# Expert layer on one core: the second expert matrix loaded by whole rows, its products regrouped, one output bank for each expert

## The chip, the cores and the metric

The kernel runs on one core of one Trainium2 chip. The metric is the device time of one execution in microseconds (us); lower is better. A program on one core has one TensorE, one VectorE (DVE), one ScalarE (ACT), one GpSimd (POOL), one SyncE (SP, which here issues most DMAs) and 16 DMA engines.

## The reference

The whole program is two transformer blocks on 256 tokens of 1024 features, float32. The change touches only its last part, the mixture of experts of the second block. There are 16 experts; each picks its 32 best tokens.

```python
def expert_choice_moe(h, p):
    cap = EC_CAPACITY * T // N_EXPERTS
    affinity = jax.nn.softmax((h @ p['router_w']).astype(jnp.float32), axis=-1)
    gates, idx = lax.top_k(jnp.swapaxes(affinity, 1, 2), cap)
    xe = jax.vmap(lambda hb, ib: hb[ib])(h, idx)
    hid = jax.nn.silu(jnp.einsum('becd,edf->becf', xe, p['exp_w1'])) * jnp.einsum('becd,edf->becf', xe, p['exp_w3'])
    ye = jnp.einsum('becf,efd->becd', hid, p['exp_w2']) * gates[..., None].astype(h.dtype)
    return jax.vmap(lambda ib, yb: jnp.zeros((T, D), yb.dtype).at[ib.reshape(-1)].add(yb.reshape(-1, D)))(idx, ye)
```

Here `exp_w1` and `exp_w3` are [1024, 2048] for each expert and `exp_w2` is [2048, 1024]. Each of the three is 8 MB, so the 16 experts read 384 MB. After the sum comes a norm of the rows, a gain, and the addition to the block's input.

## The kernel before, in words

The part in question is the function `moe` (lines 1589 to 1838). It runs after the attention block, two dense feed-forward blocks and the second mixer. Weights stay in HBM until they are used; each load of them is one DMA of 1 MB, issued by SP in `wload` (L1764), into a slot of 8 KB on each of the 128 partitions. There are 19 slots, used in turn (`RINGS`, `RING_ORDER`, `slot`), and a slot is loaded again once TensorE has used what it held. The loads of one expert are eight of `exp_w1`, eight of `exp_w3` and eight of `exp_w2`, in that order, expert after expert: 384 in all. They all go through SP's one queue in the order of the program.

For one expert, in the order of the work:

- L1779: products with `exp_w1`, then with `exp_w3`. A load holds 128 rows of 2048 numbers, one whole row of 8 KB on each partition. Four matmuls use it, one for each group g of 512 hidden columns; the stationary operand is the expert's 32 gathered tokens (`xeT`), so each matmul takes 32 columns of TensorE's array, and the four stand side by side and fill the 128 partitions of a PSUM bank: partition 32 g + token, column = hidden column inside the group.
- L1790 to L1792: silu and the gating product, on ACT and DVE, into `th` (the trace calls it mth) of 128 x 512.
- L1795 and L1797: four transposes on TensorE bring the hidden columns onto partitions (`hid`); block q takes the 128 columns q * 128 to q * 128 + 127 of every group.
- L1802 and L1804: the matrix that puts the 32 results back to their tokens with their gates, repeated four times over the 128 partitions (`pgT`).
- L1812: products with `exp_w2`, first for output columns 0 to 511, then for 512 to 1023 (`nh`). A load for half `nh` and block q takes, on each partition, four pieces of 512 numbers (2 KB): the half row of hidden column q * 128 + p of each of the four groups. Four matmuls use it, one for each group, into four groups of 32 partitions of one PSUM bank.
- L1815 and L1817: when a half is done, ACT copies the bank to SBUF (`ye`), and two matmuls, one for each half of the tokens, add it to the output sums in PSUM (`acc[t][nh]`). Their contraction over 128 partitions also adds the four groups.

```python
wv = A["exp_w2_2"][e].rearrange("(g q p) n -> q p g n", g=4, q=4)      # before
for nh in range(2):
    ns = slice(nh * 512, nh * 512 + 512)
    pe2 = psT.tile([128, 512], F32, name="tr")
    for q in range(4):
        w2t = wload(wv[q, :, :, ns], 512)
```

After the last expert come the squares of the four sums on ACT and their product with the gain on DVE (in the loop over nh, then t), the inverse root of the mean square on POOL and DVE, the residual, and four stores (L1838). Lines that go through the helper `then` stand in the trace as L1625.

Of the kernel before, what the change touches and what calls it, by code (L numbers as in the profile page):

```python
# [165 lines left out]
def _body(nc, tc, ctx, A, out):  # L166
# [42 lines left out]
    def rsqrt(ss, p, n, eps, op=ALU.add, pool=None):  # L209
        """1/sqrt(ss + eps) (or of max(ss, eps)) on [p, n]; ss may come in two parts to add."""  # L210
# [25 lines left out]
    def mean_sq_halves(x_ap, junk):  # L236
        """The mean square of a row in two parts, for rsqrt."""
        ss = small.tile([128, 2], F32, name="ssq")
        for nh in range(2):
            ns = slice(nh * 512, nh * 512 + 512)  # L240
            S.activation(junk[:, ns], x_ap[:, ns], AF.Square, scale=1.0 / 32, accum_out=ss[:, nh:nh + 1])
        return ss[:, 0:1], ss[:, 1:2]
# [5 lines left out]
    def transposes(dst_fn, src, n, dense=True):  # L248
        """PE-transpose n 128-column blocks of src; dst_fn(j0, k, ps) takes each bank's worth."""
# [8 lines left out]
    # this many of 1024 columns of a weight split have their low part from Pool  # L258
    share = [0]

    def wsplit(src, a, b, pool=None, name="w", eng=None, raw=None):
        """[a * 128, b] weights (a * b <= 1024) as a list of a (high, low) pairs of [128, b]."""
# [14 lines left out]
    def proj_tok(hT, w, kc, n0, n):  # L277
        """[128 tok, n] x 2 token tiles of h @ w[:, n0:n0+n]."""
# [13 lines left out]
    def proj_feat_acc(o, parts, hT, k0, bank0):  # L292
        """Accumulates feature-major products into o(c); the first to touch a bank starts it."""
# [11 lines left out]
    def proj_feat(hT, w, n0, n, take):  # L305
        """Feature-major [128 f, 256 tok] chunks of h @ w[:, n0:n0+n], n <= 512; take(c, ps)."""
# [14 lines left out]
    def norm_T(hT, t, x, xn, gain_bc):  # L321
        """rms norm of one token tile with a gain row, transposed and split in two parts into hT."""
# [6 lines left out]
    def in_turn(normed):  # L329
        """Both token tiles' norms ahead of what follows from the first."""  # L330
# [4 lines left out]
    def wide(w, nk, lhs, spare, done):  # L335
        """[T, D] of nk * 128 rows of w; the last rows' products go token tile by token tile, and
        done(t, two banks) follows each. lhs(k) gives the two parts [128, T]."""
# [27 lines left out]
    def ffn(xs, hT, gain, wg, wu, wd, hooks, then):  # L365
        """hooks: other work to issue before (-1) or after a block of hidden columns. hT is None where
        the norm is still to be done; then(pool, scratch) gives what follows for a finished token tile."""
# [43 lines left out]
    # ---------------------------------------------------------------- attention block  # L411
    skew = dram.tile([20, 128, 384], F32, name="skew")

    def bias_rows():
        """Bias by distance for every head (masked), once per partition, for a skewed load."""
# [14 lines left out]
    def attention(xs, hT, next_gain):  # L430
        """The block on the normed input hT; returns the normed input of the next, of gain next_gain."""
        with ExitStack() as fx:
# [55 lines left out]
            def evac_later(jobs, last=None):  # L488
                """(columns, take) projections, each block's take issued after the next block's products."""
# [7 lines left out]
            # ---- projections  # L497
# [65 lines left out]
            # ---- attention  # L563
            def softmax(lg, mx):
                """exp(lg - mx) in place; returns 1/sum."""
# [123 lines left out]
            def swept(attn):  # L689
                """Both query tiles, each head's output after the next one's logits."""  # L690
# [12 lines left out]
            def gates(i, nh):  # L703
                """1 + tanh of half the gate: twice its sigmoid."""
# [23 lines left out]
            def branch(w, kc, oT, nh, gs):  # L728
                """y += sigmoid(gate) * (o @ w), a factor 2 left in."""
# [55 lines left out]
    # ---------------------------------------------------------------- modulation  # L785
# [3 lines left out]
    def modulation(side, blocks, after=None):  # L789
        """Rows of silu(c) @ mod_w + mod_b; block 0 goes feature-major to mfm, the others to mrows, with  # L790
        the gains of the norms they meet (and a half) in them. For block 0 the
        tensor engine sums, for two vectors at once; the others are of one vector only, and their sums
        over a partition are Pool's. A generator: those start on each step, and end on the next."""
        with ExitStack() as fx:
# [17 lines left out]
            for b in blocks:  # L812
# [54 lines left out]
                # mfm[:, r, 0] = norm1_pre * (1 + scale), mfm[:, r, 1] = shift  # L867
# [7 lines left out]
    def mod_row(dst, v, eng=None):  # L875
        """dst[128, 1024] = lat modulation vector v on every partition."""
        (eng or S).dma_start(dst, mrows[2 * v:2 * v + 2, :].rearrange("(o a) n -> o (a n)", o=1).to_broadcast([128, D]))

    def norm_mod_T(hT, t, x, r, xn, us, dense=True):
        """The modulated norm of one token tile, transposed and split in two parts into hT."""  # L880
# [17 lines left out]
    # ---------------------------------------------------------------- rwkv  # L898
# [35 lines left out]
    def rwkv(rp, c, zr, zk, zv, zl, S0, alt, stage=None):  # L934
        """Recurrence over 8 heads and both directions in chunks of CH tokens. zr None: final states
        only. What stage holds is free after the recurrence. zk and zv are overwritten. Returns (states, y in PSUM, v, r * sum of k_mod * r_k)."""
# [182 lines left out]
        # inverses of the unit triangular 32-blocks: partition (d, block, t, head) holds one of them  # L1119
# [29 lines left out]
        # the off-diagonal blocks, T21 = T22 N21 T11 (or its mirror), from right to left  # L1149
# [101 lines left out]
    def context_states(side):  # L1251
        """In two steps: the norm, then the rest."""
# [24 lines left out]
    # ---------------------------------------------------------------- hyena filter  # L1277
# [6 lines left out]
    def hyena_filter(spec, dft, side):  # L1284
        """spec[:, 0] the real and spec[:, 1] the sine part of the filter's transform, with the weights
        of the inverse; row 0 of the sine part holds the real part at the highest frequency."""
# [302 lines left out]
    def moe(xs, w1, po, m2p, xr, rw, m3c, a2c, last):  # L1589
        with ExitStack() as fx:  # L1590
# [176 lines left out]
            for e in range(NE):  # L1767
# [26 lines left out]
                for q in range(4):  # L1794
                    PE.transpose(pt[:, q, :], th[:, q * 128:(q + 1) * 128], ident)  # L1795
# [101 lines left out]
```

## Time and profile before

| | |
|---|---|
| device time, median of 3 runs | 2231.14 us (2227.08 to 2231.18) |
| profiled execution, from its first to its last instruction | 2224.2 us |
| what the runs' median has on top of that span | 6.9 us |
| TensorE busy | 1826.4 us, 82% of the span |
| DVE busy, ACT busy, POOL busy | 887.3, 589.9, 335.4 us |
| expert loads | 384, of 1024 KB each |
| first and last issue of an expert load | 1194.0 and 2196.1 us |

The page gives no device time of the profiled execution itself beside its span. The rows further down come from the trace of that one execution. Times in them are in us from the start of the span, if nothing else is said. PE is TensorE's matmuls, PEld its loads of stationary weights, SPq what SP's queue does. One float32 matmul stands as two records of PE. A number in brackets behind a row is the idle time of the engine just before it, and what ended it. "DMA ring<-exp_w" is the landing of an expert load.

### The profile page before, as it was taken

What the parts mean: (1) busy time and instruction counts of PE and PEld (TensorE: products, weight loads), DVE (VectorE), ACT (ScalarE), POOL (GpSimd) and SP (SyncE); (2) the same over time, 40 slices, a digit from 0 to 9 for tenths busy, and PEclk for the clock granted to TensorE, in tenths of its full rate; (3) what the DMA queues carried; (4) which work ended last, traced back from release to release, by engine and by line L of the source; (5) the groups of instructions that cost most, each with busy time, mean ns of one, the idle gap of its engine ahead of it and who ended that gap; (6) DMA issues with size and microseconds to landing.
All of it is one profiled execution on the core that took longest, in us unless ns stands there. A gap on an engine that the chain in (4) does not pass through costs nothing.

```text
span 2224.2 us, 28420 instructions
## 1 busy us (share of the span) xinstructions
PE 1826.4 (82%) x11441; PEld 1108.2 (50%) x11442; DVE 887.3 (40%) x1611; ACT 589.9 (27%) x954; POOL 335.4 (15%) x332
## 2 busy tenths in 40 slices
PE   7999999999988899898999876766766666667775
PEld 5888877777768877888687521111111111111111
DVE  4577855865757765777647410000000000000001
ACT  3345443544436544453314200000000000000001
POOL 2111013210325540235233200000000000000000
PEclk9999989999989999989889887677677787777667
DMA  8654545444448855424336899999999999999997
GB/s 296 222 167 134 171 131 171 136 145 121 132 143 270 280 185 182 141 81 113 115 105 220 314 409 410 410 409 406 407 407 406 407 407 410 410 411 409 406 407 302
DMA packets 237046, 600.95 MB, mean 270 GB/s; under 512 B 35384, under 2 KB 91217, under 8 KB 204146
## 3 DMA queue, kind: packets, MB, share of 16 engines
q1 hardware_dynamic: 200464, 551.89, 67.6%
q0 software_dynamic: 10496, 36.08, 4.9%
q10 hardware_dynamic: 25954, 11.16, 1.9%
q8 instruction: 90, 1.47, 0.3%
q14 instruction: 42, 0.34, 0.0%
HBM read 593.25 MB, written 9.75 MB: 271 GB/s over the span
## 4 chain that ended last, share of the span: by engine, by line
DMA 42%; PE 41%; DVE 8%; ACT 3%; issue 3%; POOL 1%; SPq 0%; ACTq 0%; DVEq 0%; POOLq 0%
DMA ring<-exp_w 39%; PE mm L302 4%; PE mm L299 3%; PE mm L288 3%; PE mm L301 3%; PE mm L287 3%; PE mm L289 3%; DVE wl L246 2%; PE mm L346 2%; PE mm L345 2%; PE mm L349 2%; PE px L1779 1%; DMA wraw<-w_in 1%; ACT wh L245 1%; PE tr L1812 1%
## 5 line engine op out<-in xcount | busy, mean ns | idle before, releaser
L1779 PE MATMUL px<-ring,xeT 128*32 128x512 f32 x2048 | 370.0, 812 | 181.9 <-DMA ring<-exp_w 181.7
L246 DVE TENSOR_TENSOR wl<-wraw,wh 128x1024 fp32r<-128x1024 f32 (+2 forms) x243 | 317.5, 1307 | 174.2 <-ACT wh L245 169.9
L245 ACT ACTIVATE wh<-wraw 128x1024 fp32r<-128x1024 f32 (+2 forms) x243 | 254.5, 1048 | 352.5 <-PE mm L301 143.5
L1779 PEld LDWEIGHTS px<-ring,xeT 128*32 128x32 f32 x2048 | 48.7, 123 | 474.6 <-DMA ring<-exp_w 440.4
L302 PE MATMUL mm<-hh,wl 128*128 128x256 f32 x912 | 266.6, 294 | 18.6 <-DVE wl L246 16.6
L299 PE MATMUL mm<-hh,wh 128*128 128x256 f32 x912 | 265.7, 292 | 2.1 <-ACT hh L245 2.1
L301 PE MATMUL mm<-hl,wh 128*128 128x256 f32 x912 | 264.1, 290 | 1.7 <-DVE hl L246 1.6
L1791 DVE SCALAR_TENSOR_TENSOR mth<-mth,px 128x512 f32<-128x512 f32 x16 | 11.0, 687 | 580.4 <-ACT mth L1790 580.4
L1812 PE MATMUL tr<-ring,hid 128*32 128x512 f32 x1024 | 166.8, 758 | 77.8 <-DMA ring<-exp_w 65.1
L302 PEld LDWEIGHTS mm<-hh,wl 128*128 128x128 f32 x912 | 178.6, 196 | 33.2 <-DVE wl L246 21.4
L299 PEld LDWEIGHTS mm<-hh,wh 128*128 128x128 f32 x912 | 179.6, 197 | 11.4 <-issue 7.6
L301 PEld LDWEIGHTS mm<-hl,wh 128*128 128x128 f32 x912 | 179.5, 197 | 6.6 <-issue 3.9
L1815 ACT ACTIVATE ye<-tr 128x512 f32<-128x512 f32 x32 | 19.1, 597 | 566.7 <-PE tr L1812 566.7
L1625 POOL TENSOR_SCALAR rsz<-ss 128x1 f32<-128x1 f32 x2 | 0.6, 302 | 952.9 <-ACT ring L1625 952.8
L288 PE MATMUL mm<-wl,hh 128*128 128x512 f32 (+2 forms) x320 | 127.9, 400 | 2.3 <-DVE wl L246 2.0
L1812 PEld LDWEIGHTS tr<-ring,hid 128*32 128x32 f32 x1024 | 26.4, 124 | 203.4 <-DMA ring<-exp_w 143.8
L289 PE MATMUL mm<-wh,hl 128*128 128x512 f32 (+2 forms) x320 | 124.6, 390 | 0.0
L287 PE MATMUL mm<-wh,hh 128*128 128x512 f32 (+2 forms) x320 | 117.7, 400 | 6.7 <-DVE wi L525 3.6
L1817 PE MATMUL mm<-ye,pgT 128*128 128x512 f32 x128 | 92.8, 865 | 24.0 <-ACT ye L1815 24.0
L1792 DVE SCALAR_TENSOR_TENSOR mth<-mth,px 128x512 f32<-128x512 f32 x16 | 11.0, 687 | 253.0 <-PE px L1779 253.0
L1790 ACT ACTIVATE mth<-px 128x512 f32<-128x512 f32 x16 | 9.5, 597 | 283.5 <-PE px L1779 283.5
L1817 PEld LDWEIGHTS mm<-ye,pgT 128*128 128x128 f32 x128 | 30.1, 260 | 88.4 <-ACT ye L1815 63.7
(756 smaller groups left out, 2792.4 us busy)
## 6 DMA issues: line engine op xcount, KB each, us to landing
ring<-exp_w SPq DMA_DIRECT2D x384, 1024.0 KB
wraw<-w_in SPq DMA_DIRECT2D x107, 512.0 KB
mraw<-mod_w POOLq DMA_DIRECT2D x48, 512.0 KB, 5.1
wraw<-ffn_w_gate SPq DMA_DIRECT2D x44, 512.0 KB
wraw<-ffn_w_up SPq DMA_DIRECT2D x44, 512.0 KB
wraw<-ffn_w_down SPq DMA_DIRECT2D x44, 512.0 KB
wraw<-w_out SPq DMA_DIRECT2D x11, 512.0 KB
skew<-bd POOLq DMA_DIRECT2D x1, 3840.0 KB, 27.7
```

Of the source, the lines that this page charges most:

```text
L245: S.activation(dst_h, src, AF.Copy)
L246: (eng or V).tensor_tensor(dst_l, src, dst_h.bitcast(F32), op=ALU.subtract)
L287: PE.matmul(ps[t], hh[:, k, sl], wh, start=(k == 0), stop=False)
L288: PE.matmul(ps[t], hh[:, k, sl], wl, start=False, stop=False)
L289: PE.matmul(ps[t], hl[:, k, sl], wh, start=False, stop=(k == kc - 1))
L299: PE.matmul(o(c), wh[:, cs], hh[:, k, :], start=(k == 0 and bank0(c)), stop=False, skip_group_check=True)
L301: PE.matmul(o(c), wh[:, cs], hl[:, k, :], start=False, stop=False, skip_group_check=True)
L302: PE.matmul(o(c), wl[:, cs], hh[:, k, :], start=False, stop=(k == KC - 1), skip_group_check=True)
L345: PE.matmul(acc[t][nh], fh[:, sl], wh[:, ns], start=(k == 0), stop=False)
L1779: PE.matmul(ps[32 * g:32 * g + 32, :], xeT[:, k, es], wt[:, 0, g * 512:(g + 1) * 512], start=(k == 0), stop=(k == KC - 1), skip_group_chec ...
L1812: PE.matmul(pe2[32 * g:32 * g + 32, :], hid[:, q, 32 * g:32 * g + 32], w2t[:, g, :], start=(q == 0), stop=(q == 3), skip_group_check=True)
L1817: PE.matmul(acc[t][nh], pgT[:, t * 128:(t + 1) * 128], ye, start=(e == 0), stop=(e == NE - 1))
```

## The change

In `moe`, the second matrix is read with another numbering of its rows. Hidden row g * 512 + 4 p + 2 h + j goes to partition p; one load, for a group g and a half h, takes the two neighbouring rows j = 0 and 1 for each partition, which is 8 KB in one piece. The next load, of the other h, takes the 8 KB that lie between those pieces. So that the hidden values match, the transposes take every fourth column of `th`. Each load now serves four matmuls of one group, for both j and both halves of the output; they stand in the four groups of 32 partitions of one bank: partitions 0 to 63 hold the two partial sums of the first half, 64 to 127 those of the second. The bank is copied once for each expert, and each of the four scatter matmuls contracts over 64 partitions. The number of loads, their size and the number of matmuls stay as they were.

```diff
-                    PE.transpose(pt[:, q, :], th[:, q * 128:(q + 1) * 128], ident)
+                    PE.transpose(pt[:, q, :], th[:, q::4], ident)
...
-                wv = A["exp_w2_2"][e].rearrange("(g q p) n -> q p g n", g=4, q=4)
-                for nh in range(2):
-                    ns = slice(nh * 512, nh * 512 + 512)
-                    pe2 = psT.tile([128, 512], F32, name="tr")
-                    for q in range(4):
-                        w2t = wload(wv[q, :, :, ns], 512)
-                        for g in range(4):
-                            PE.matmul(pe2[32 * g:32 * g + 32, :], hid[:, q, 32 * g:32 * g + 32], w2t[:, g, :],
-                                      start=(q == 0), stop=(q == 3), skip_group_check=True)
-                    ye = tmp.tile([128, 512], F32, name="ye")
-                    S.activation(ye, pe2, AF.Copy)
-                    for t in range(2):
-                        PE.matmul(acc[t][nh], pgT[:, t * 128:(t + 1) * 128], ye, start=(e == 0), stop=(e == NE - 1))
+                wv = A["exp_w2_2"][e].rearrange("(g p h j) n -> g h p (j n)", g=4, h=2, j=2)
+                pe2 = psT.tile([128, 512], F32, name="tr")
+                for g in range(4):
+                    for h in range(2):
+                        w2t = wload(wv[g, h], 512)
+                        for j in range(2):
+                            for nh in range(2):
+                                c = nh * 2 + j
+                                PE.matmul(pe2[32 * c:32 * c + 32, :], hid[:, 2 * h + j, 32 * g:32 * g + 32],
+                                          w2t[:, j * 2 + nh, :], start=(g == 0 and h == 0), stop=(g == 3 and h == 1),
+                                          skip_group_check=True)
+                ye = tmp.tile([128, 512], F32, name="ye")
+                S.activation(ye, pe2, AF.Copy)
+                for t in range(2):
+                    for nh in range(2):
+                        r = slice(nh * 64, nh * 64 + 64)
+                        PE.matmul(acc[t][nh], pgT[r, t * 128:(t + 1) * 128], ye[r, :], start=(e == 0), stop=(e == NE - 1))
```

All other lines of the diff take out comments.

On SP, at the end of its queue, the form of the expert loads (the numbers are partitions, then pieces and numbers in a piece; mrows is the row of the gain, loaded after them), the difference:

```order
-L1764 DMA ring<-exp_w_2 128x2048 x16
-L1764 DMA ring<-exp_w_2 128x4x512 x8
-L1764 DMA ring<-exp_w_2 128x2048 x16
-L1764 DMA ring<-exp_w_2 128x4x512 x8
+L1764 DMA ring<-exp_w_2 128x2048 x384
 L877 DMA ring<-mrows 128x1024
-L1838 DMA out<-ring 128x512 x4
+L1844 DMA out<-ring 128x512 x4
```

The loads of the second matrix had four pieces of 512 numbers on a partition; now all 384 loads are of one form, one piece of 2048 numbers, and nothing else moves on this queue.

On TensorE, from the second matrix of one expert to that of the next (L1815 is the line of those products now, L1823 that of the scatter), the difference:

```order
-L1812 MATMUL tr<-ring,hid 32x512 x16
-L1817 MATMUL mm<-ye,pgT 128x512 x2
-L1812 MATMUL tr<-ring,hid 32x512 x16
-L1817 MATMUL mm<-ye,pgT 128x512 x2
+L1815 MATMUL tr<-ring,hid 32x512 x32
+L1823 MATMUL mm<-ye,pgT 128x512 x4
 L1779 MATMUL px<-ring,xeT 32x512 x36
```

The scatter of the first half stood between the products of the two halves; now both halves are scattered after all eight loads.

On ACT, the end of the program: first before,

```order
667 L1815 ACTIVATE ye<-tr 128x512
668 L1625 ACTIVATE ring,ss_14971<-mm 128x512 x2
669 L1815 ACTIVATE ye<-tr 128x512
670 L1625 ACTIVATE ring,ss_14971<-mm 128x512 x2
671 L1625 ACTIVATE ring<-ring,rsr 128x512
```

and now:

```order
667 L1819 ACTIVATE ye<-tr 128x512
668 L1625 ACTIVATE ring,ss_14923<-mm 128x512 x4
669 L1625 ACTIVATE ring<-ring,rsr 128x512
```

Two of the four squares stood ahead of the last copy of an output bank; now all four stand behind it.

## Rows read from the trace of the kernel before

**Rows 1.** The page: DMA activity (tenths) and rate in 40 slices of 55.6 us.

```profile
DMA  8654545444448855424336899999999999999997
GB/s 296 222 167 134 171 131 171 136 145 121 132 143 270 280 185 182 141 81 113 115 105 220 314 409 410 410 409 406 407 407 406 407 407 410 410 411 409 406 407 302
```

**Rows 2.** The page: the chain that ended last, by line.

```profile
DMA ring<-exp_w 39%; PE mm L302 4%; PE mm L299 3%; PE mm L288 3%; PE mm L301 3%; PE mm L287 3%; PE mm L289 3%; DVE wl L246 2%; PE mm L346 2%; PE mm L345 2%; PE mm L349 2%; PE px L1779 1%; DMA wraw<-w_in 1%; ACT wh L245 1%; PE tr L1812 1%
```

**Rows 3.** Stretches: us, busy time (records) by engine, granted clock, DMA share, GB/s.

```profile
1262.00:1300.00 38.00, 36.09 (x256) 13.80 (x254) 6.24 (x14) 5.85 (x12) 0.00 (x0) 0.97 0.93 357
1300.00:2192.00 892.00, 603.04 (x3019) 106.56 (x3018) 36.00 (x72) 31.44 (x58) 0.00 (x0) 0.74 1.02 408
2106.00:2168.00 62.00, 44.25 (x206) 7.61 (x206) 2.51 (x5) 2.17 (x4) 0.00 (x0) 0.67 1.02 408
2132.00:2134.00 2.00, 2.00 (x12) 0.44 (x12) 0.00 (x0) 0.00 (x0) 0.00 (x0) 0.50 1.04 385
```

**Rows 4.** TensorE in time: landings of first-matrix loads, start us, us.

```profile
2094.71 0.16 PEld L1779 LDWEIGHTS px<-ring,xeT 128*32 128x32 f32 x8 [2.33 <-DMA ring<-exp_w]
2097.21 0.20 PEld L1779 LDWEIGHTS px<-ring,xeT 128*32 128x32 f32 x8 [2.35 <-DMA ring<-exp_w]
...
2107.18 0.20 PEld L1779 LDWEIGHTS px<-ring,xeT 128*32 128x32 f32 x8 [2.33 <-DMA ring<-exp_w]
2107.18 1.94 PE L1779 MATMUL px<-ring,xeT 128*32 128x512 f32 x8 [1.43 <-DMA ring<-exp_w]
```

**Rows 5.** TensorE in time: landings of second-matrix loads, in three experts.

```profile
2087.23 0.16 PEld L1812 LDWEIGHTS tr<-ring,hid 128*32 128x32 f32 x8 [2.34 <-DMA ring<-exp_w]
...
2143.44 0.16 PEld L1812 LDWEIGHTS tr<-ring,hid 128*32 128x32 f32 x8 [1.50 <-DMA ring<-exp_w]
2146.16 0.16 PEld L1812 LDWEIGHTS tr<-ring,hid 128*32 128x32 f32 x8 [2.56 <-DMA ring<-exp_w]
2148.79 0.20 PEld L1812 LDWEIGHTS tr<-ring,hid 128*32 128x32 f32 x8 [2.48 <-DMA ring<-exp_w]
```

**Rows 6.** DMA, 2150 to 2170 us: packets, then the queue's share of 16 engines.

```profile
DMA packets 1149, 8.38 MB, mean 419 GB/s; under 512 B 127, under 2 KB 127, under 8 KB 127
q1 hardware_dynamic: 1148, 8.36, 100.9%
```

**Rows 7.** DMA, 2124 to 2144 us: the same.

```profile
DMA packets 3749, 7.75 MB, mean 388 GB/s; under 512 B 119, under 2 KB 119, under 8 KB 3699
q1 hardware_dynamic: 3748, 7.73, 103.9%
```

**Rows 8.** SP's queue in time: an issue of the first form, and one of the second.

```profile
2166.25 0.33 SPq L1764 DMA_DIRECT2D ring<-exp_w  x1
2176.23 8.01 SPq L1764 DMA_DIRECT2D ring<-exp_w  x1
```

**Rows 9.** The end in time: from the last landing on.

```profile
2210.30 1.06 PE L1812 MATMUL tr<-ring,hid 128*32 128x512 f32 x8 [1.49 <-DMA ring<-exp_w]
2211.49 0.60 ACT L1815 ACTIVATE ye<-tr 128x512 f32<-128x512 f32 x1 [4.68 <-PE tr L1812]
2212.14 1.98 PE L1817 MATMUL mm<-ye,pgT 128*128 128x512 f32 x4 [0.78 <-ACT ye L1815]
2213.31 0.60 ACT L1625 ACTIVATE ring<-mm 128x512 f32<-128x512 f32 x1 [1.22 <-PE mm L1817]
2214.22 0.60 ACT L1625 ACTIVATE ring<-mm 128x512 f32<-128x512 f32 x1 [0.23 <-PE mm L1817]
2214.94 0.69 DVE L1625 TENSOR_TENSOR ring<-mm,ring 128x512 f32<-128x512 f32 x1 [0.23 <-ACT ring L1625]
```

**Rows 10.** The same view, one half earlier: scatter of the first half.

```profile
2202.30 3.78 PE L1817 MATMUL mm<-ye,pgT 128*128 128x512 f32 x4 [0.78 <-ACT ye L1815]
```

**Rows 11.** What SP's queue waited for, 1300 to 2190 us: total us, times, longest.

```profile
SPq L1764 <- DMA ring<-exp_w: 390.1, 200, 2.8
```

**Rows 12.** Groups by line, 1230 to 2224 us: the transposes' weight loads; busy us, mean ns.

```profile
L1795 PEld LDWEIGHTS tr<-ident,mth 128*128 128x128 f32 x64 | 8.8, 174 | 33.0 <-DVE mth L1792 33.0
```

## The prediction

> **What bounds the kernel now.** I read the page first, in slices of time. In the first half the DMA engines are about half busy; from the 24th slice on, 1280 us, they are at 9 tenths or more, and the rate stays at 406 to 411 GB/s up to the last slice [rows 1]. The chain of waits says the same: 39% of the span is the landing of expert loads, and the next line has 4% [rows 2]. The busy time by stretches shows that TensorE is not the limit there: 603 us busy of 892, while the DMA share is 1.02 [rows 3]. So from 1300 us on one queue of 1 MB loads sets the time, and the end comes a fixed tail after the last landing.
>
> Then I looked for what differs between the loads of one expert, since the change touches only a third of them. TensorE in time shows landings as the ends of its waits. Loads of the first matrix (the third has the same form) land 12.47 us apart over five loads, from 2094.71 to 2107.18: 2.494 us each [rows 4]. Loads of the second matrix land 2.72 and 2.63 us apart [rows 5]. The DMA queue shows why. In 20 us of first-form loads it moves 1149 - 127 = 1022 packets of 8 KB at a share of 100.9% [rows 6]: 1.009 x 16 x 20 / 1022 = 316 ns of one engine each. In 20 us of second-matrix loads it moves 3699 - 119 = 3580 packets of 2 KB and 50 of 8 KB at 103.9% [rows 7]: (332.5 - 15.8) / 3580 = 88.5 ns each, 354 ns for the same 8 KB. The pieces cost engine time, 12% more of it, and the rate falls from 419 to 388 GB/s [rows 6, 7]. SP also stands longer in an issue, 8.01 us against 0.33 [rows 8], but since the share is over 100% all the while, no engine runs dry for that.
>
> **The change part by part.**
>
> *Rows of 8 KB.* All 384 loads become one form, which the order on SP shows. I take the new loads at the first form's 2.494 us. The period of an expert is 2148.79 - 2087.23 = 61.56 us between last landings [rows 5]; 24 loads at 2.494 are 59.86; difference 1.70. By the mean rate of the whole stretch, 25.17 MB / 0.408 = 61.68 us [rows 3], it is 1.82; by the rates of rows 6 and 7, 8.389 / 0.388 - 8.389 / 0.419 = 1.60; by the two gaps alone 8 x 0.18 = 1.45 [rows 5]. I take 1.75, nearest to the two that cover whole experts, and 1.45 to 1.82 as bounds. Fifteen experts (the second to the last) are loaded with the queue full: 15 x 1.75 = **26.2 us gained**.
>
> *The first expert.* Its second matrix is loaded while TensorE, busy 36.09 of 38 us, still works off the slots that filled before it began, and the rate is 357 GB/s [rows 3]. If slots set the pace nothing is gained there, if the DMA does, 1.7. I take 0.8.
>
> *The tail.* Before, half of the scatter was done while loads still came. After the last landing came four products, one copy (2211.49), two scatter matmuls (2212.14 on, 1.98 for both, 0.99 each), and two squares at 1.17 and 2.08 us after the scatter's start [rows 9]. Now four matmuls and four squares follow. The squares go by half, then by tokens; the matmuls by tokens, then by half; so the second square needs the third matmul: 3 x 0.99 + 0.18 = 3.15 us, and with 0.91 us a square the third starts at 4.06, the fourth at 4.97. That is 4.97 - 2.08 = **2.9 us lost**. If the two matmuls of 64 rows run side by side, the third ends at 1.98 and the loss is 1.9. With TensorE at 1.2 GHz (3.78 us for two matmuls [rows 10]) the squares start at 2.07, 5.85, 6.76 and 7.67: 5.6 lost.
>
> *What TensorE does later in each expert.* The first half's scatter now waits for all eight loads, and the next expert's first products stand behind two more matmuls: 2 us at the higher clock, 3.8 at the lower. Behind them wait landed loads, and SP if no slot comes free. There are 19 slots, and SP's largest wait is for landings of older loads [rows 11]; a load's products take 1.06 to 1.94 us [rows 4, 9] of the 2.494, so this is caught up. I count 0. If this cover went, it would show as the third rival below.
>
> *Small things.* One copy of a bank fewer for each expert (0.60 us on ACT [rows 9]) is off the path, as ACT waits for TensorE. The transposes read their 128 columns with stride 4. The trace has no such read; its weight loads take 174 ns [rows 12], 0.55 us an expert. Bounds: nothing, and four times as long, 1.65 us more for an expert. Either way it lies in the time in which TensorE waits for the next landing; 0, and for a gain there is no reason. The number of product matmuls, their tile of 32 columns and their spread over four column groups are the same, so their cost is unchanged.
>
> Sum: -26.2 - 0.8 + 2.9 = -24.1 us. Against the profiled execution that is a span of 2224.2 - 24.1 = 2200.1. The median of the runs lies 6.9 above that span, and I carry this over: 2231.1 - 24.1 = **2207.0 us**.
>
> **The rivals.**
>
> *The row length is not all of it (chance 0.06).* The slower loads also differ in that they skip: 2 KB out of every 4 KB, in four places 2 MB apart. The new ones skip too, 8 KB out of every 16 KB. If half of the difference comes from that, 15 x 0.87 = 13.1 is gained, less 2.9: 2220.9. For it: nothing in the trace separates length from skipping. Against it: the extra is in the packets' own time, and 88.5 against 316 / 4 = 79 ns is what a fixed part of some 13 ns on each packet would give. The Trainium skill, in "DMA: Bandwidth & Descriptors", section "Why small descriptors are slow", gives a fixed overhead of 3 cycles beside one cycle for each 32 bytes, which by my estimate is 268 cycles for four pieces and 259 for one row, 3.5%, and would give a time near this rival's. The trace shows more than that, the 12% above.
>
> *The loads are no faster (0.04).* Pieces of 2 KB would already run at what the queue gives, and the difference between the forms would come from elsewhere, such as where this matrix lies in HBM. Then only the tail is left: 2231.1 + 2.9 = 2234.0, no change by measure. Rows 6 and 7 speak against it, at the same length of stretch and no other traffic. This is what a rule says that speaks against the change: the Trainium skill, "DMA: Bandwidth & Descriptors", "Specifications", puts the smallest transfer for line rate at 512 bytes, and "Rules for kernel authors" asks for 1 MiB in a DMA on 128 partitions, which both versions have. Here the trace disagrees: 388 against 419 GB/s.
>
> *TensorE becomes the bound (0.05).* At 1.2 GHz, eight records of products take 1.94 us [rows 4], so an expert needs 24 x 1.94 + 2 x 3.78 = 54.1 us of the 59.9 that remain, and transposes and waits for ACT and DVE must fit in 5.8. If they take 1 us more than that, an expert gains 0.75 in place of 1.75 and the tail costs 5.6: 2231.1 - 11.2 + 5.6 = 2225.5. The granted clock speaks against it: it was 0.50 only in short stretches, 0.67 to 0.74 over long ones, and 0.97 where TensorE had no pauses [rows 3]; a TensorE that is pressed does not stay slow.
>
> *Rows with gaps are slower than pieces (0.03).* In the new loads the 128 partitions start 16 KB apart, in the old ones 4 KB, in the first form 8 KB. If streams at that distance meet in the same part of HBM, a load takes longer; it is slower than before as soon as a load needs over 2.494 + 1.75 / 8 - 2.9 / 120 = 2.69 us. At most I would expect the time of the 2 MB over which a load is spread, 4.99 us: 120 x (4.99 - 2.71) + 2.9 = 276 us more, 2507. Against it: the old loads skip as well, and the fixed part above explains them without it. [...]
>
> **How the numbers follow.** The forecast has 0.82. Its own bounds: best 15 x 1.82 + 1.7 - 1.9 = 27.1 gained, 2204.0; worst 15 x 1.45 + 0 - 5.6 = 16.2 gained, 2214.9. Single runs lay up to 4.1 under the median, so I set the range from 2200 to 2217, which leaves out the rivals' 0.18. A measurement of this kernel can tell about 0.2%, 4.5 us, from no change. Faster by more than that: the forecast, the first and the third rival, 0.93. Within it: the second, 0.04. Slower: the fourth, 0.03.
>
> **What the profile after would show.** Right: landings 2.49 us apart over all 24 loads, an expert's period near 59.9 us, the rate at 418 to 421 GB/s from 1300 us on, no 2 KB packets in the expert loads, every issue on SP near 0.33 us, four squares after the last scatter, and some 2.9 us more from the last landing to the end. Wrong: second-matrix landings still over 2.6 us apart (first, second or fourth rival, told apart by the size), or waits for landings gone from TensorE in the last experts (the third).

## Result, and the profile after

The changed kernel takes 2200.06 us in the median of 5 runs (2197.78 to 2210.83), against 2229.69 before (5 runs, 2225.24 to 2231.18): a ratio of 0.988, 95% interval 0.9857 to 0.9903. The profiled execution has a span of 2209.1 us and a device time of 2210.83, the slowest of the five.

The page of the kernel after, DMA activity and rate in 40 slices, then the chain by line:

```profile
DMA  8654545453448855533425799999999999999996
GB/s 298 223 170 133 171 134 162 141 149 115 143 123 270 279 196 175 148 90 90 144 73 182 304 397 420 420 420 420 419 420 420 420 420 420 420 420 419 420 420 275
...
DMA ring<-exp_w 40%; PE mm L302 4%; PE mm L299 4%; PE mm L301 4%; PE mm L287 3%; PE mm L288 3%; PE mm L289 3%; DVE wl L246 2%; PE mm L346 2%; PE mm L345 2%; PE mm L349 2%; DMA wraw<-w_in 1%; ACT wh L245 1%; PE px L1779 1%; PE tr L1106 1%
```

Where the rate swung between 406 and 411 GB/s [rows 1], it is now 419 or 420 from the 25th slice to the last but one. The landing of expert loads is still the longest part of the chain.

By stretches (columns as in [rows 3]), the whole expert stage after the first expert:

```profile
1300.00:2170.00 870.00, 571.68 (x3038) 96.25 (x3030) 35.21 (x71) 23.71 (x45) 0.00 (x0) 0.74 1.01 420
```

TensorE in time, landings of second-matrix loads in two experts (they answer to [rows 5]):

```profile
2059.83 0.16 PEld L1815 LDWEIGHTS tr<-ring,hid 128*32 128x32 f32 x8 [1.70 <-DMA ring<-exp_w]
...
2069.81 0.20 PEld L1815 LDWEIGHTS tr<-ring,hid 128*32 128x32 f32 x8 [2.33 <-DMA ring<-exp_w]
...
2119.69 0.20 PEld L1815 LDWEIGHTS tr<-ring,hid 128*32 128x32 f32 x8 [1.89 <-DMA ring<-exp_w]
...
2129.66 0.20 PEld L1815 LDWEIGHTS tr<-ring,hid 128*32 128x32 f32 x8 [2.29 <-DMA ring<-exp_w]
```

Four loads take 9.98 and 9.97 us, 2.494 each, as the first matrix did all along [rows 4]; from last landing to last landing an expert takes 2129.66 - 2069.81 = 59.85 us.

What SP's queue waited for, 1300 to 2190 us (as in [rows 11]), and an issue of a second-matrix load (as in [rows 8]):

```profile
SPq L1764 <- DMA ring<-exp_w: 734.7, 348, 3.5
...
2156.04 0.33 SPq L1764 DMA_DIRECT2D ring<-exp_w  x1
```

SP's long issues are gone, and most of its time is waiting for older loads to land: 734.7 of 890 us.

The end in time (it answers to [rows 9]):

```profile
2191.06 1.93 PE L1815 MATMUL tr<-ring,hid 128*32 128x512 f32 x8 [0.56 <-DMA ring<-exp_w]
2193.12 0.60 ACT L1819 ACTIVATE ye<-tr 128x512 f32<-128x512 f32 x1 [36.45 <-PE tr L1815]
2193.77 3.79 PE L1823 MATMUL mm<-ye,pgT 64*128 64x512 f32 x8 [0.78 <-ACT ye L1819]
2195.88 0.60 ACT L1625 ACTIVATE ring<-mm 128x512 f32<-128x512 f32 x1 [2.16 <-PE mm L1823]
...
2198.17 0.59 ACT L1625 ACTIVATE ring<-mm 128x512 f32<-128x512 f32 x1
...
2198.74 0.60 ACT L1625 ACTIVATE ring<-mm 128x512 f32<-128x512 f32 x1
```

From the last landing to the end there are now 2209.1 - 2191.06 = 18.0 us, against 2224.2 - 2210.30 = 13.9 before. The first issue of an expert load was at 1194.0 us before and at 1201.1 in this execution, in code that the change does not touch; so I compare from there: to the last landing it was 1016.3 us before and is 990.0 now, 26.3 less, and the tail takes 4.1 back. Of that time, the 14 periods from the second expert's last landing to the sixteenth's were 2210.30 - 1344.42 = 865.9 us and are 2191.06 - 1348.49 = 842.6.

### The profile page after: what moved, and what is told of

The parts are those of the page before. It is cut to its first block, busy times and chain, and to the rows that moved or that the text cites. A ratio compares the mean times of both kernels' runs of the same rounds, so it can differ in the third digit from the quotient of the medians.

```text
span 2209.1 us, 28416 instructions
## 1 busy us (share of the span) xinstructions
PE 1799.4 (81%) x11441; PEld 1104.3 (50%) x11442; DVE 885.2 (40%) x1611; ACT 580.9 (26%) x938; POOL 335.4 (15%) x332
## 4 chain that ended last, share of the span: by engine, by line
DMA 43%; PE 41%; DVE 8%; issue 3%; ACT 3%; POOL 1%; ACTq 0%; SPq 0%; DVEq 0%; POOLq 0%
DMA ring<-exp_w 40%; PE mm L302 4%; PE mm L299 4%; PE mm L301 4%; PE mm L287 3%; PE mm L288 3%; PE mm L289 3%; DVE wl L246 2%; PE mm L346 2%; PE mm L345 2%; PE mm L349 2%; DMA wraw<-w_in 1%; ACT wh L245 1%; PE px L1779 1%; PE tr L1106 1%
## 5 line engine op out<-in xcount | busy, mean ns | idle before, releaser
L1779 PE MATMUL px<-ring,xeT 128*32 128x512 f32 x2048 | 362.3, 799 | 185.1 <-DMA ring<-exp_w 185.1
L1815 PE MATMUL tr<-ring,hid 128*32 128x512 f32 x1024 | 184.6, 827 | 96.2 <-DMA ring<-exp_w 83.6
L1819 ACT ACTIVATE ye<-tr 128x512 f32<-128x512 f32 x16 | 9.6, 598 | 557.7 <-PE tr L1815 557.7
L1815 PEld LDWEIGHTS tr<-ring,hid 128*32 128x32 f32 x1024 | 27.1, 129 | 234.6 <-DMA ring<-exp_w 202.8
L288 PEld LDWEIGHTS mm<-wl,hh 128*128 128x128 f32 x320 | 60.7, 190 | 19.8 <-DVE wl L246 3.2
L287 PEld LDWEIGHTS mm<-wh,hh 128*128 128x128 f32 x320 | 58.7, 190 | 21.2 <-issue 7.2
```

What stands on the lines that cost most here:

```text
L287: PE.matmul(ps[t], hh[:, k, sl], wh, start=(k == 0), stop=False)
L288: PE.matmul(ps[t], hh[:, k, sl], wl, start=False, stop=False)
L1779: PE.matmul(ps[32 * g:32 * g + 32, :], xeT[:, k, es], wt[:, 0, g * 512:(g + 1) * 512], start=(k == 0), stop=(k == KC - 1), skip_group_chec ...
L1815: PE.matmul(pe2[32 * c:32 * c + 32, :], hid[:, 2 * h + j, 32 * g:32 * g + 32], w2t[:, j * 2 + nh, :], start=(g == 0 and h == 0), stop=(g = ...
```

## Experiments

Theory 1: the number of pieces in which a load is moved sets its time. Rival, theory 2: the old loads were slow in part because they skip half of each row and jump between four distant places. The first four kernels ran on one chip with the kernel before (2223.08 us, 17 runs there). A row of the view by stretches, 1350 to 2170 us, stands for each; 25.17 MB divided by its rate is an expert's period.

**The changed kernel again (r_after).**

> The changed kernel once more, beside the others on one chip. Both theories: about 0.988 of the kernel before, 24 to 30 us less; 24 landings an expert at 2.49 us; from the last landing to the end about 3 us more than before with TensorE at 2.4 GHz in the end, 4 us more at 1.2 GHz.

2203.76 us, ratio 0.9908 (0.9878 to 0.9939).

```profile
1350.00:2170.00 820.00, 529.47 (x2820) 88.31 (x2812) 34.11 (x68) 21.50 (x41) 0.00 (x0) 0.75 1.01 420
...
2185.92 1.49 PE L1815 MATMUL tr<-ring,hid 128*32 128x512 f32 x8 [0.56 <-DMA ring<-exp_w]
2188.20 1.99 PE L1823 MATMUL mm<-ye,pgT 64*128 64x512 f32 x8 [0.79 <-ACT ye L1819]
...
2191.37 0.60 ACT L1625 ACTIVATE ring<-mm 128x512 f32<-128x512 f32 x1
```

Here the first issue was at 1195.6 and the last landing at 2185.92: 990.3 us, 26.0 less than before. The tail is 2201.7 - 2185.92 = 15.8 us, 1.9 more than before. Together 24.1 us less. TensorE's clock was not the same in the two tails. By stretches, the last scatter in the execution above, then here:

```profile
2193.77:2197.55 3.78, 3.78 (x8) 1.18 (x8) 0.69 (x1) 0.69 (x2) 0.00 (x0) 0.50 0.00 0
...
2188.20:2190.20 2.00, 1.99 (x8) 0.69 (x8) 0.12 (x1) 0.69 (x2) 0.00 (x0) 1.00 0.00 0
```

The granted clock is 0.50, which is 1.2 GHz, in the first, and 1.00, 2.4 GHz, here.

**Pieces without skipping, second matrix (e1_w2_2k).** The slots are padded so that four pieces of 512 numbers cannot merge.

```diff
-                        w2t = wload(wv[g, h], 512)
+                        w2t = wpieces(wv[g, h])
...
+            def wpieces(src):
+                r = slot().rearrange("p (s m) -> p s m", m=520)[:, :, 0:512]
+                with tc.issue_after(last):
+                    nc.sync.dma_start(r, src.rearrange("p (s n) -> p s n", n=512))
+                return r
```

> The changed kernel with its second-matrix loads cut into four pieces of 2 KB on each partition: the same rows of HBM, the same products, the same tail; the pieces only land 32 bytes apart in a slot, so that they cannot be one. One slot fewer (18). Theory 1 (the number of pieces costs, some 13 ns of an engine each): second-matrix landings back at 2.71 us, 26 us slower than the changed kernel, and slower than the kernel before by the tail alone, 3 to 4 us. Theory 2 (half of the old cost came from skipping 2 KB out of every 4 KB in four places 2 MB apart, which is not done here): landings at 2.60, 13 us slower than the changed kernel. If all of it came from skipping: no slower.

2220.0 us, ratio 0.999 (0.9974 to 1.0006), an interval that holds 1. The regrouped products and the scatter are those of the changed kernel, so the changed kernel's gain came from the form of the loads. View by stretches, then landings in time:

```profile
1350.00:2170.00 820.00, 538.01 (x2768) 91.23 (x2760) 32.79 (x66) 21.50 (x41) 0.00 (x0) 0.71 1.03 411
...
2069.18 0.16 PEld L1821 LDWEIGHTS tr<-ring,hid 128*32 128x32 f32 x8 [2.49 <-DMA ring<-exp_w]
...
2079.83 0.20 PEld L1821 LDWEIGHTS tr<-ring,hid 128*32 128x32 f32 x8 [2.42 <-DMA ring<-exp_w]
```

Four landings in 10.65 us are 2.66 each, between the 2.71 of theory 1 and the 2.60 of theory 2. A period is 25.17 / 0.411 = 61.2 us: of the 1.8 us between 59.9 (420 GB/s) and 61.7 (408), 1.3 are back. By the medians it is 16.2 us slower than the changed kernel, between the 26 and the 13 that the theories gave; from first issue to last landing its profiled execution takes 1012.6 us, 22.3 more than the one above. Its first two experts also took about 4.7 us longer than those of the changed kernel (first issue to the second expert's last landing); it has one slot fewer, and I did not separate that.

**Pieces without skipping, the other two matrices (e2_w13_2k).** The same `wpieces` for the first and third matrix; the second stays whole.

> The changed kernel with the loads of the first and third matrix in four pieces of 2 KB, each load still one unbroken MB of HBM with nothing skipped; 18 slots. Theory 1: 16 landings of each expert at 2.71 us in place of 2.49, 15 x 16 x 0.22 = 52 us slower than the changed kernel, 2 to 4 more from the first expert. Theory 2: with nothing skipped, at most half of that, 26 us, or none.

2243.29 us, ratio 1.0092 (1.0066 to 1.0118), 39.5 us over the changed kernel.

```profile
1350.00:2170.00 820.00, 559.36 (x2702) 91.95 (x2700) 32.58 (x65) 20.51 (x39) 0.00 (x0) 0.66 1.04 401
...
2049.45 0.16 PEld L1785 LDWEIGHTS px<-ring,xeT 128*32 128x32 f32 x8 [1.89 <-DMA ring<-exp_w]
...
2060.14 0.20 PEld L1785 LDWEIGHTS px<-ring,xeT 128*32 128x32 f32 x8 [2.44 <-DMA ring<-exp_w]
...
2028.78 0.20 PEld L1821 LDWEIGHTS tr<-ring,hid 128*32 128x32 f32 x8 [1.67 <-DMA ring<-exp_w]
...
2036.28 0.20 PEld L1821 LDWEIGHTS tr<-ring,hid 128*32 128x32 f32 x8 [2.35 <-DMA ring<-exp_w]
```

Loads that lie in HBM without a gap slow down to 10.69 / 4 = 2.67 us when they are cut. The second matrix, whole here, lands (2036.28 - 2028.78) / 3 = 2.50 us apart in the same 18 padded slots, so the slots alone do not make the landings slow. So most of the cost is the pieces, but 39.5 is again between the 52 and the 26 that the theories gave.

**Two rows of 4 KB (e3_w2_4k).** Transposes of neighbouring columns again, whole rows from two places:

```diff
-                wv = A["exp_w2_2"][e].rearrange("(g p h j) n -> g h p (j n)", g=4, h=2, j=2)
+                wv = A["exp_w2_2"][e].rearrange("(g h j p) n -> g h p j n", g=4, h=2, j=2)
...
```

> The changed kernel with second-matrix loads of two whole rows from two places, 4 KB each, and transposes of neighbouring columns. Theory 1: two packets of 13 + 151 ns are 328 ns for 8 KB, against 316 and 354, so a third of the old difference is back: second-matrix landings at 2.57 us, 9 us slower than the changed kernel. Theory 2: whole rows, nothing skipped inside a row, each load covers its range of HBM without gaps in two places: as fast as the changed kernel or faster.

2201.12 us, ratio 0.9907 (0.9881 to 0.9933), not told apart from the changed kernel by time; the 9 us more of theory 1 did not come.

```profile
1350.00:2170.00 820.00, 538.21 (x2788) 87.74 (x2780) 34.10 (x68) 21.50 (x41) 0.00 (x0) 0.72 1.02 416
...
2049.34 0.17 PEld L1815 LDWEIGHTS tr<-ring,hid 128*32 128x32 f32 x8 [1.14 <-DMA ring<-exp_w]
...
2062.10 0.20 PEld L1815 LDWEIGHTS tr<-ring,hid 128*32 128x32 f32 x8 [2.33 <-DMA ring<-exp_w]
```

Five landings in 12.76 us are 2.552 each, against 2.57 expected of theory 1. So the landing time goes 2.494, 2.55, 2.66 with one, two and four pieces for 8 KB. Most of the 9 us are in the loads all the same: from first issue to last landing this execution takes 997.4 us, 7.1 more than the changed kernel's. They don't show in its span, 2200.1 us, because its first issue came at 1186.5, 9.1 us earlier than there, in code that is the same in both.

SP's issues grow with the pieces too: up to 8.06 us in e1 and 4.65 here, against 0.33 to 0.72 in the changed kernel. No run cuts loads without making issues longer. That the issues do not set the time is argued, not shown by a run: the DMA engines' share stays at 1.02 to 1.04 in all of these stretches.

**Half rows that lie near each other (e8_near).** The kernel before, but a load takes the half rows of four neighbouring rows, 4 KB apart; the transposes take every fourth column, as in the changed kernel:

```diff
-                wv = A["exp_w2_2"][e].rearrange("(g q p) n -> q p g n", g=4, q=4)
+                wv = A["exp_w2_2"][e].rearrange("(g p q) n -> g p q n", g=4, q=4)
...
```

> The kernel before with half rows of four neighbouring hidden rows in a load, 4 KB apart, in place of four places 2 MB apart; still 2 KB pieces that skip 2 KB each. It tells what the last quarter of the old cost is, which cutting alone did not bring back (period of an expert 61.55 us before, 61.05 with cut pieces, 59.85 with whole ones). If skipping half rows costs it: a period near 61.55 us. If the distance of the four places costs it: near 61.05.

One execution, 2221.78 us.

```profile
1350.00:2170.00 820.00, 537.51 (x2736) 96.46 (x2728) 32.76 (x66) 29.25 (x54) 0.00 (x0) 0.77 1.02 408
...
2062.71 0.16 PEld L1812 LDWEIGHTS tr<-ring,hid 128*32 128x32 f32 x8 [1.41 <-DMA ring<-exp_w]
2065.43 0.16 PEld L1812 LDWEIGHTS tr<-ring,hid 128*32 128x32 f32 x8 [2.56 <-DMA ring<-exp_w]
2068.14 0.16 PEld L1812 LDWEIGHTS tr<-ring,hid 128*32 128x32 f32 x8 [2.55 <-DMA ring<-exp_w]
```

2.72 and 2.71 us apart at 408 GB/s, as before. So bringing the four places together gains nothing; half rows cost about 0.05 us a load more than whole rows cut into as many pieces. That it is the skipping is what is left over: the pieces of e1 also lie apart in their slots, and no run has half rows laid down like that.

**The order of the scatter (e5_scatter_order).** For the tail: are four matmuls of 64 rows as quick as two of 128 because neighbours use different rows?

```diff
-                for t in range(2):
-                    for nh in range(2):
+                for nh in range(2):
+                    for t in range(2):
```

> The changed kernel with the scatter in the order half of the output, then half of the tokens, so that neighbouring matmuls mostly contract over the same 64 partitions. If two matmuls on different 64 partitions run side by side (theory 1 of the tail), the eight records at the end take about 3.0 us at 2.4 GHz or 5.7 at 1.2 in place of 2.0 or 3.8, since only the middle pair can overlap; the tail is up to 1 us longer, landings stay at 2.49 us. If they do not overlap and the four are quick for another reason, the eight records take as long as in the changed kernel.

One execution, 2203.77 us; from first issue to last landing 990.2 us, and a tail of 15.8, as in r_after.

```profile
2188.51 1.99 PE L1823 MATMUL mm<-ye,pgT 64*128 64x512 f32 x8 [0.79 <-ACT ye L1819]
2189.66 0.60 ACT L1625 ACTIVATE ring<-mm 128x512 f32<-128x512 f32 x1 [1.21 <-PE mm L1823]
...
2190.52 0.60 ACT L1625 ACTIVATE ring<-mm 128x512 f32<-128x512 f32 x1 [0.17 <-PE mm L1823]
```

The eight records take 1.99 us, not 3.0. By the expectation the four matmuls would then be quick for another reason, but their records say that they do run side by side. The last scatter by line, before and here (ns of one record: least, median, most), then TensorE here from 2188.50 to 2188.55 us:

```profile
L1817 PE MATMUL mm<-ye,pgT x4: 592/592/697, 2212.1 to 2213.5; 128*128 128x512 f32 x4
L1823 PE MATMUL mm<-ye,pgT x8: 589/589/693, 2188.5 to 2189.9; 64*128 64x512 f32 x8
...
2188.51 0.71 PE L1823 MATMUL mm<-ye,pgT 64*128 64x512 f32 x2 [0.79 <-ACT ye L1819]
```

A record over 64 partitions takes as long as one over 128: 589 against 592 ns. Two of them begin within these 0.05 us and are over 0.71 us after the first began. So the eight are four pairs, and take the time of the four records of [rows 9]. The two of a pair belong to two matmuls: the first square, which needs the first matmul alone, waited until 2189.66, when two pairs were done. Over all experts, before and in the changed kernel, the line's busy time halves while the mean of a record stays:

```profile
L1817 PE MATMUL mm<-ye,pgT 128*128 128x512 f32 x128 | 92.8, 865 | 24.0 <-ACT ye L1815 24.0
L1823 PE MATMUL mm<-ye,pgT 64*128 64x512 f32 x128 | 46.0, 853 | 12.7 <-ACT ye L1819 12.7
```

What falls is that only neighbours could pair. In this order the first two matmuls use the same 64 partitions, and the second square needs the second of them. It did not follow the first square, which ended at 2190.26, but waited for TensorE until 2190.52, when the scatter was over (2188.51 + 1.99 = 2190.50). So the first matmul's partner was not its neighbour but a later one, on the other 64 partitions.

**Rows of 16 KB for the second matrix (e6_w2_16k), then for all (e7_16k).** If a piece has a price, longer ones should gain more. Nine slots of 16 KB; the second matrix in loads of 2 MB, then also the other two, with the features renumbered:

```diff
-                wv = A["exp_w2_2"][e].rearrange("(g p h j) n -> g h p (j n)", g=4, h=2, j=2)
+                wv = A["exp_w2_2"][e].rearrange("(g p h j) n -> g p (h j n)", g=4, h=2, j=2)
...
+                            w2k = wload2(A[nm][e, k * 128:(k + 2) * 128, :].rearrange("(p j) n -> p (j n)", j=2))
```

> The changed kernel with second-matrix loads of 2 MB, four whole rows (16 KB) in one piece on each partition, in 9 slots of 16 KB; the other loads stay 1 MB each, two to a slot. If the cost of a piece holds on (11 to 13 ns of an engine each, 0.05 to 0.07 us on a load's landing), a second matrix takes 8 pieces fewer on each engine for each MB pair: 4 x 0.1 us less an expert, a period of about 59.5 us in place of 59.85, 5 us less in all, and a tail 1 to 2 us longer since the last landing brings twice the products. Rival: a row of over 8 KB is moved as pieces of 8 KB or less, and the period stays 59.85.

> All loads of 2 MB with 16 KB in one piece on each partition: two neighbouring rows of the first and third matrix, with the feature rows of the gathered tokens, of the router and of the norm's gain and offset renumbered to match. If the cost of a piece holds on, three times the gain of the kernel with only the second matrix so: a period of about 58.7 us, 15 x 1.15 = 17 us less than the changed kernel, minus a tail 1 to 2 us longer. Rival: larger pieces are cut again or something else limits the 16 engines at 421 GB/s, and the period stays 59.85; the tail then makes it slightly slower than the changed kernel.

e6: 2203.12 us, 0.9894 (0.9869 to 0.9919); e7: 2199.66 us, 0.9882 (0.9851 to 0.9913), against 2229.28 of the kernel before there. No more than the change itself. In e6 the rate is 422 GB/s from 1350 to 2170 us, a period of 59.6 us against the 59.5 expected. In e7 the stage is quicker and the loads stay whole; stretches before and after 1300 us, then the packets from 1800 to 2000 us and the queue's share (columns as in [rows 6]):

```profile
1190.00:1290.00 100.00, 82.37 (x483) 59.28 (x481) 49.84 (x94) 31.01 (x65) 25.92 (x27) 0.85 0.67 276
1300.00:2165.00 865.00, 517.15 (x3058) 114.80 (x3058) 36.25 (x73) 23.66 (x45) 0.00 (x0) 0.80 1.01 427
...
DMA packets 5866, 85.37 MB, mean 427 GB/s; under 512 B 655, under 2 KB 655, under 8 KB 655
q1 hardware_dynamic: 5859, 85.26, 100.4%
```

5866 - 655 = 5211 packets of 16 KB at 1.004 x 16 x 200 / 5211 = 617 ns: the rival, that they are cut again, falls, and 427 GB/s is a period of 58.9 us. What was won is lost at the start, where 276 GB/s (279 in e6) moved in the 100 us before 1290, against 314 in the changed kernel, and in the tail, 19.4 us in e7 against 15.8:

```profile
1190.00:1290.00 100.00, 83.66 (x461) 59.32 (x459) 54.73 (x103) 33.70 (x68) 25.95 (x27) 0.86 0.82 314
```

**Slots in the order in which they come free (e9_16k_order), and a shorter end (e10_16k_last).**

```diff
-RING_ORDER = (0, 1, 2, 3, 4, 5, 6, 7, 8)
+RING_ORDER = (3, 1, 8, 7, 6, 4, 5, 0, 2)
...
-                    w2t = wload2(wv[g])
+                    if e < NE - 1 or g < 3:
+                        w2t = wload2(wv[g])
+                        parts = [w2t[:, 0:4], w2t[:, 4:8]]
+                    else:
+                        parts = [wload(wv[g][:, h * 2048:h * 2048 + 2048], 512) for h in range(2)]
```

The first part alone is e9, both are e10.

> The kernel with 16 KB rows in all loads, its 9 slots now taken in the order in which the memory below them comes free (by the issues of the changed kernel), in place of the order of their numbers. Theory: with 16 KB rows an expert takes 1.0 us less (58.9 us against 59.85), but 100 us after the first issue 26.3 MB were there against 31.0, 11 us behind, as the second and third load waited 21 and 25 us for their slots. With the order mended most of that comes back: 29 to 31 MB after 100 us, and 5 to 10 us less than that kernel. Rival: a slot of 16 KB comes free later whatever the order, since it lies over more of the old tiles and goes only when both its rows are used; then it stays near 26 MB and the time does not change.

> The same with the last 2 MB of the last expert as two loads of 1 MB with 8 KB rows, so that half of their products are done when the last MB lands. The tail after the last landing goes from 19.4 us back to 16 to 18, 1 to 2 us less than with the order alone; nothing else moves.

On one chip, with the kernel before at 2224.61 us: e9 2191.76 us, ratio 0.9857 (0.9836 to 0.9879); e10 2185.8 us, ratio 0.9824 (0.9808 to 0.984). View by stretches of e10, and the last landing and scatter of e9 in time:

```profile
1190.00:1290.00 100.00, 83.81 (x488) 56.04 (x488) 47.56 (x91) 28.99 (x62) 25.98 (x27) 0.86 0.79 312
1300.00:2165.00 865.00, 524.25 (x3010) 114.61 (x3014) 36.45 (x73) 23.08 (x44) 0.00 (x0) 0.79 1.00 426
...
2166.86 3.64 PE L1841 MATMUL tr<-ring,hid 128*32 128x512 f32 x16 [1.27 <-DMA ring<-exp_w]
2171.28 1.99 PE L1849 MATMUL mm<-ye,pgT 64*128 64x512 f32 x8 [0.78 <-ACT ye L1845]
```

The order brings the start back to 312 GB/s, and the stage stays at 426. After 100 us from the first issue 29 MB (of 1024 KB) were there in both, between e7's 26.3 and the changed kernel's 31.0. From first issue to last landing e9 takes 981.3 us, 5.5 less than e7, inside the 5 to 10 that were expected; by time the two are not told apart, as their intervals overlap. The tail is 2184.7 - 2166.86 = 17.8 us in e9 and 14.9 in e10, below the 16 to 18 expected. The medians of e9 and e10 differ by 6.0 us, more than the expected 1 to 2; single executions of e9 lie between 2186.5 and 2199.23, and what the rest is was not tried. e10's interval lies below both intervals of the change (0.9857 to 0.9903 and 0.9878 to 0.9939), so this version is faster than both kernels, by 1.8% of the one before. Its profiled execution is 18.2 us shorter than that of the changed kernel in r_after; of these, 8.1 lie ahead of the first issue (1187.5 against 1195.6), and only the other 10.1 in the expert stage.

## Why the prediction was right, point by point

*What bounds the kernel.* Right. The landing of loads set the end before and after, and the time moved with it: 26.3 and 26.0 us less from first issue to last landing in two executions, against the 26.2 + 0.8 that were forecast. Over the last 14 periods it is (865.9 - 842.6) / 14 = 1.66 us for each, against the 1.75 taken.

*Rows of 8 KB.* Right in size: 2.494 us a landing, a period of 59.85 us against 59.86, 420 GB/s, and no long issue on SP. The cause was named too simply. "The pieces cost engine time" holds for about 1.3 of the 1.8 us between the periods (e1, and e2 at the other loads); the remaining 0.4 or 0.5 us are left to reading half rows (e8), which the new loads don't do. So the first rival had a mechanism that is there, with a quarter of the difference and not half of it, and its price for the new loads was nil: pieces of 8 KB that skip 8 KB land as quickly as those that skip nothing.

*The other rivals.* The second falls with e1 and e2: with the same matrix in the same place, cutting loads costs the time. The fourth falls with the landings above. The third did not come up: TensorE still waits for a landing before most loads, busy 571.68 us of 870, at a mean granted clock of 0.74, as before [rows 3].

*The tail.* Forecast 2.9 us, 1.9 with the small matmuls side by side, 5.6 at 1.2 GHz; measured 1.9 in one execution and 4.1 in the other. Two steps were off. "3 x 0.99 + 0.18" lets the four matmuls follow one another, while they run in pairs (e5), the case that the prediction gave 1.9 us. And "0.91 us a square" is no price of a square: in [rows 9] the second square waited for a matmul, and a square that waits for nothing starts 0.57 us after the one ahead (2198.74 against 2198.17). So in r_after the last square began 2191.37 - 2188.20 = 3.17 us after the scatter's start, where the case with pairs had 3.98. That 1.9 came out even so is luck: the last products took 1.49 us against 1.06, and the part behind the last square 0.35 us more than before. In the execution with 4.1 the last products (1.93 us) and the scatter (3.79) ran at 1.2 GHz. The last square began 2198.74 - 2193.77 = 4.97 us after the scatter's start, the very number that was forecast, but by a slower clock, matmuls in pairs and shorter squares: errors that cancel.

*Small things.* The transposes' weight loads with stride 4 took 214 ns in the mean against 174 [rows 12], 0.16 us an expert, inside the waits.

*The sum.* Forecast 2207.0 us, 24.1 less. The ratio of the forecast is 0.9892, inside both measured intervals. The forecast lies 6.9 us above the median of 2200.06, which is at the very edge of the stated range (2200 to 2217) and below the 2204.0 that the sum gave as its best; only the allowance for the spread of single runs covers it. The medians fell by 29.6 us in the first comparison and by 19.3 in the second, while the part from the first issue on fell by 22.2 and 24.1 in the profiled executions. So the sum was near for the part that it describes, and that the first comparison's median still lies inside the range is in part luck. Carrying over 6.9 us as what "lies above that span" was wrong as a description: in the profiled execution after, device time and span differ by 2210.83 - 2209.1 = 1.7. With as much on top, the profiled execution before would have been one of the quicker ones, near 2226; its own device time is not on record. Executions of one program differ by some 10 us, and part of that stands ahead of the experts: the first issue was at 1201.1 and 1195.6 us in two executions of the changed kernel.

## What to carry to other kernels

Where one queue of large loads sets the time, compare the landings of its forms and divide the queue's share by its packets. A difference in packet time for the same bytes tells what other sizes will do: for pieces of 4 KB a third of the old difference was expected, a landing of 2.57 us, and 2.55 was measured. Take the size of the effect from the landings: the packets took 12% longer [rows 6, 7], the landings 5 to 9% [rows 5]. Choose the numbering of a contraction so that each partition reads whole neighbouring rows; any order of the summed index will do if the other operand is brought into the same order, here by a stride in a transpose. When records of an engine overlap, compare the time of one record as well as that of the group. Before you count on longer rows, look at what they do to the first fill of the slots and to the work left after the last landing.

## What was not expected of the hardware

- Float32 matmuls over different 64 partitions ran in pairs, side by side: eight records of 589 ns in 1.99 us, against four of 592 in 1.98 over 128 partitions. They paired also where neighbours in the program use the same 64 partitions.
- Half rows (2 KB out of every 4) cost more than their number of pieces: 2.71 us a load against 2.66 with as many pieces and nothing skipped, while skipping 8 KB after every 8 KB cost nothing, 2.494 either way.
- A row of 16 KB is moved as one packet, 617 ns against 316 for 8 KB, and lifts the rate from 420 to 427 GB/s.
- Now and then a landing came 1.4 us late, as here in the changed kernel (3.91 us apart in place of 2.49). In this execution the periods that end with the sixth, the eleventh and the sixteenth expert are 61.3 or 61.4 us, those of the others from the third on 59.8 or 59.9. Its cause wasn't tried.

```profile
2142.14 0.16 PEld L1779 LDWEIGHTS px<-ring,xeT 128*32 128x32 f32 x8 [2.34 <-DMA ring<-exp_w]
2146.05 0.20 PEld L1779 LDWEIGHTS px<-ring,xeT 128*32 128x32 f32 x8 [3.75 <-DMA ring<-exp_w]
```
